# Decode key pages: loads from SyncE's queue, addressed by a register, in place of GpSimd's indirect row gathers

## The chip, the cores and the metric

The kernel runs on 1 core of one Trainium2 chip. The metric is the device time of one execution in microseconds (us), lower is better. The engines are named as in the profile: PE is TensorE (its weight loads are shown apart as PEld), DVE is VectorE, ACT is ScalarE, POOL is GpSimd, and SP is SyncE, which here only issues transfers; "SPq" in a row is such an issue.

## The reference

One step of a one-layer decoder trunk, in float32, for a prompt of 1024 tokens and for 8 sample sequences of one new token each. Prompt and samples share the weights. Each sample has 256 past tokens, whose keys and values lie in a cache of pages of 128 tokens; a page table names two pages for each sample. The part that matters here is the keys of the samples' differential attention:

```python
k_past = cache_k[l][page_table].reshape(Bd, past, H_A, 2 * DK_A)      # 8 samples, 256 tokens, 4 heads, 128
k_all = jnp.concatenate([k_past.astype(ka_d.dtype), ka_d], axis=1)
oa_d = diff_attention(qa_d, k_all, v_all, pos_d, kpos_d, rel_bias, lam)

def probs(qi, ki):
    s = jnp.einsum('bqhd,bkhd->bhqk', qi, ki).astype(f32) * scale + bias
    return jax.nn.softmax(jnp.where(mask, s, neg), axis=-1)

attn = probs(q1, k1) - lam * probs(q2, k2)
```

Around it stand the projections, the same attention and a retention over the prompt, a cross-attention into a memory, an MLP and several norms.

## The kernel before

The 1032 tokens (1024 of the prompt, 8 of the samples) are columns; weights come as "units" of 128 x 1024 floats. Each operand is split into a high part and a remainder (`wh`/`wl`, `UH`/`UL`, `KA`/`KB`, `VH`/`VL`), and each product is three matmuls. The program is written once, in one order; a scheduler places each engine's instructions from it, and within the attention stage (`pin[0] = True`) TensorE's are kept in the order written.

The attention stage runs from about 233 to 460 us. A loop over `g` from -4 to 39 takes the four heads, ten steps each (`items`): scores (`sp`, L1000), transposes (`trA`), weighting (`av`). Between them it feeds in a "filler": the projections of queries and keys of the next heads (`qkp`), and behind these the decode, `decode_steps`. Values of a head are fetched by SP into `vraw`, cast by ACT into `VH` (L974), and the remainder `VL` is formed on POOL (L976). Keys of a head are cast into `KA` by ACT (L948), the remainder `KB` is formed on DVE (L950), and both halves are copied across partitions by transfers that POOL issues (L949, L951). Weight units are loaded by SP into a pool of three buffers with the tag `raw`, cast by ACT (L128, `wh_u`) and their remainder is formed on DVE (L129, `wl_u`).

`decode_steps` builds an index tile `idk` of 128 x 16: column k holds 128 times the k-th page number plus the row. `fetch(x)` loads one of eight key tiles, each of two halves of 128 x 512 floats (256 KB), one page a half. The cache is laid out so that a page is 128 consecutive rows of 2 KB. Tiles 0 to 3 are fetched ahead, into the buffers of spent weight units; tiles 4 to 7 are fetched as the matmuls `dsc` consume tiles, into the `raw` buffers that vraw, a broadcast row (`rbh`) and, for the last one, tile 4 have used. Every half is one indirect DMA issued by POOL (`gather`, L858): POOL makes the row addresses, and the data goes over POOL's queue, q0. The other users of q0 in this stage are the copies of KA and KB and two loads of `UL` and `UH`.

SP issues its transfers strictly in order: one that waits for a buffer holds back what stands behind it. Its transfers carry one of eight semaphores in turn (`DMAHW0` to `DMAHW7`, those of POOL's queue `DMASW0` to `DMASW7`). Behind the attention stage the out-projection uses units that are loaded late in the stage (`raw_o`, L1396, and `raw_u`) and the stored head outputs `OP`, read back as `op` (L1258).

Of the kernel before, what the change touches and what calls it, by code (L numbers as in the profile page):

```python
# [12 lines left out]
I32 = mybir.dt.int32  # L13
AF = mybir.ActivationFunctionType
ALU = mybir.AluOpType
# [4 lines left out]
P = 128  # L20
# [28 lines left out]
def decoder_step(ctx: ExitStack, tc: tile.TileContext, i: dict, o: dict):  # L49
    nc = tc.nc  # L50

    def pool(name, bufs=1, space=None, side=None):
        if space is None:
            return tc.tile_pool(name=name, bufs=bufs, reuse_waits="tile", side=side)
        if space is PSUM:
            return tc.tile_pool(name=name, bufs=bufs, space=space, reuse_waits="tile")
        return tc.tile_pool(name=name, bufs=bufs, space=space)
# [111 lines left out]
    def bcast_rows(row_ap, p, n):  # L169
        return bass.AP(tensor=row_ap.tensor, offset=row_ap.offset, ap=[[0, p], [1, n]])  # L170
# [215 lines left out]
    with pool("a") as A:  # L386
# [250 lines left out]
        A = r_front.enter_context(pool("r", side="right"))  # L637
# [79 lines left out]
        for t in range(8):  # L717
# [33 lines left out]
            op = PS.tile([P, 512], F32, tag="op", name=f"op_{t}", bufs=2)  # L751
# [95 lines left out]
    def rep_rows(A, dt, src, nf, dst, nm, b0=0):  # L847

        for b in range(b0, b0 + nf // 4):
# [4 lines left out]
                nc.tensor.transpose(tp[:, x * P : x * P + P], ex.rearrange("p s g -> p (s g)"), ident)  # L854
            nc.scalar.copy(dst[:, b * 512 : b * 512 + 512], tp)

    def gather(raw, src, idx, k):
        nc.gpsimd.indirect_dma_start(  # L858
            out=raw, out_offset=None, in_=src, in_offset=bass.IndirectOffsetOnAxis(ap=idx[:, k : k + 1], axis=0)
        )  # L860
# [22 lines left out]
    with pool("b") as A:  # L883
# [243 lines left out]
        def decode_steps():  # L1127
# [8 lines left out]
            for j in range(2):  # L1136
                nc.vector.tensor_tensor(idx[:, 4 * j : 4 * j + 4], idx[:, 4 * j : 4 * j + 4],
                                        pt[:, j : j + 1].to_broadcast([P, 4]), op=ALU.add)
            idk = A.tile([P, 16], I32, tag="idk", name="idk")
            pos = A.tile([P, 1], I32, tag="pos", name="pos")  # L1140
            nc.sync.dma_start(idk, bcast_rows(i["page_table"], P, 16))
            nc.sync.dma_start(pos, i["pos"])
            nc.vector.tensor_scalar(idk, idk, 128.0, None, ALU.mult)
            nc.vector.tensor_tensor(idk, idk, pos.to_broadcast([P, 16]), op=ALU.add)
            sel = A.tile([64, 32], F32, tag="sel", name="sel")
            nc.sync.dma_start(sel, i["sel"])
            hm = A.tile([64, 5], F32, tag="hm", name="hm")
# [9 lines left out]
            raws2 = {}  # L1157

            def fetch(x):
                if x < 8:  # L1160
                    if x < 4:

                        raws2[x] = G.tile([P, 1024], F32R, tag="wl" if x % 2 else "wh", name=f"ck_0_{x}", bufs=RING).bitcast(F32)
                    else:
                        raws2[x] = G.tile([P, 1024], F32, tag="raw", name=f"ck_1_{x - 4}", bufs=3)
                    for y in range(2):
                        gather(raws2[x][:, y * 512 : y * 512 + 512], i["cache_kT"], idk, 4 * (x % 4) + 2 * y + x // 4)

            for x in range(4):
                fetch(x)  # L1170
                yield
# [101 lines left out]

        filler = head_proj(0)
        decode = decode_steps()

        def fill(n):
# [50 lines left out]
        for g in range(-4, 40):  # L1328
            h, x = divmod(g, 10)
# [70 lines left out]
            if g in UNITS_AT:  # L1400
                x = len(us_out)
# [5 lines left out]
        while len(us_out) < 4:  # L1407
            x = len(us_out)
# [622 lines left out]
    with pool("e") as A, pool("e_ps", space=PSUM) as PS:  # L2031
# [61 lines left out]
        for n, (ft, c) in enumerate(order):  # L2093
# [13 lines left out]
            x = xq[ft // 4, c][:, ft % 4, :]  # L2107
# [133 lines left out]
    with pool("acc", side="right") as AC, pool("rd", side="right") as RD, pool("w") as A, pool("w_ps", space=PSUM) as PS:  # L2241
# [105 lines left out]
        for g in range(4):  # L2347
# [26 lines left out]
            for new, qs, ps_ in parts:  # L2374
# [23 lines left out]
                for n, (q, p, c) in enumerate(steps):  # L2398
# [9 lines left out]
                    y = C[INTO[q]][:, p, cq]  # L2408
# [71 lines left out]
def _bucket(n):  # L2480
    n = np.maximum(n, 0)
    nf = np.maximum(n, 1).astype(np.float32)
    large = 16 + (np.log(nf / np.float32(16)) / np.float32(np.log(8.0)) * np.float32(16)).astype(np.int32)
    return np.where(n < 16, n, np.minimum(large, 31))


def _constants():
    f = np.float32
    c = {}
    c["ident"] = np.eye(P, dtype=f)  # L2490
    lg = np.log(f(1.0) - f(2.0) ** (f(-5.0) - np.arange(4, dtype=f))).astype(f)
    inv = (f(10000.0) ** (-np.linspace(0.0, 1.0, 32, dtype=f))).astype(f)
    pos = np.concatenate([np.arange(NT), np.full(P, 256)]).astype(f)
    ang = (pos[:, None] * inv[None, :]).astype(f)
    cos, sin = np.cos(ang), np.sin(ang)
    j = np.arange(P, dtype=f)
    dq = np.exp((j + 1)[:, None] * lg[None, :])
    dk = np.exp((127 - j)[:, None] * lg[None, :]) * f(0.125)
    rot = np.zeros((9, P, 2, 2, 4, 2, 32), f)
    for t in range(9):  # L2500
        cs, sn = cos[t * P : t * P + P], sin[t * P : t * P + P]
        for x, w in ((0, dq), (1, dk)):
            if t == 8:
                w = np.full((P, 4), 0.125 if x else 1.0, f)
            for h in range(4):
                for half in range(2):
                    rot[t, :, 0, x, h, half] = cs * w[:, h : h + 1]
                    rot[t, :, 1, x, h, half] = (sn if half else -sn) * w[:, h : h + 1]
    c["rot"] = rot.reshape(9, P, 1024)
    m = np.zeros((P, 4, P), f)  # L2510
    for h in range(4):
        m[:, h, :] = np.where(j[None, :] >= j[:, None], np.exp(f(-128.0) * lg[h]), 0)
    c["maskM"] = m.reshape(P, 512)
    rd = np.zeros((P, 2, 2), f)
    hs = np.zeros((P, 32), f)
    for p in range(2):
        for e in range(2):
            rd[64 * e : 64 * e + 64, p, 0] = np.exp(f(128.0) * lg[2 * p + e])
            rd[64 * e : 64 * e + 64, p, 1] = np.exp(lg[2 * p + e])
            hs[64 * e : 64 * e + 64, e] = 1  # L2520
    c["rdec"], c["hsel"] = rd, hs
    rel = 1023 - np.arange(BIASW)
    oh = np.zeros((33, BIASW), f)
    b = _bucket(rel)
    for x in range(BIASW):
        if rel[x] >= 0:
            oh[b[x], x] = -1
        else:
            oh[32, x] = 1
    c["onehot"] = oh  # L2530
    od = np.zeros((32, 257), f)
    od[_bucket(256 - np.arange(257)), np.arange(257)] = -1
    c["onehot_dec"] = od
    r = np.arange(64)
    c["sel"] = (r[:, None] % 32 == np.arange(32)[None, :]).astype(f)
    c["hm"] = np.concatenate([(r[:, None] % 32 // 8 == np.arange(4)[None, :]), r[:, None] >= 32], 1).astype(f)
    c["pos"] = np.arange(P, dtype=np.int32)[:, None]
    pp = np.arange(P)
    sg = (pp[None, :] // 16 == np.arange(8)[:, None]).astype(f)
    c["selg"], c["selgt"] = sg, np.ascontiguousarray(sg.T)  # L2540
    c["blk"] = (pp[None, :] // 16 == pp[:, None] // 16).astype(f)
    c["idxbase"] = ((pp % 16)[:, None] * 4 + np.arange(8)[None, :] % 4).astype(np.int32)
    return c


def _layout(x):
# [39 lines left out]
    d["cmk"] = a["cache_mem_k"].reshape(P, 16, 1024)  # L2586
    d["cmv"] = a["cache_mem_v"].reshape(P, 16, 1024)
    d.update(_constants())
    return {k: np.ascontiguousarray(v) for k, v in d.items()}

# [36 lines left out]
```

## Time and profile before

| | us |
|---|---|
| median of 3 runs | 1489.31 (1488.1 to 1490.61) |
| the profiled execution | 1496.69 |
| its span, first to last instruction | 1494.8 |
| granted TensorE clock, mean over the span | 0.995 |

Times in views are microseconds from the start of the span. A row of a timeline gives start, duration, engine, line, operation, output <- inputs, count, and in brackets the idle time of the engine ahead of it and what ended it. A row of stretches gives the busy time of PE, PEld, DVE, ACT and POOL, then the granted clock, the mean busy share of the 16 DMA engines and GB/s. A row of a tile's group gives the shortest, median and longest duration in ns. SP's queue before, around the places that the change touches, from its timeline:

```profile
373.03 0.32 SPq L937 DMA_DIRECT2D M<-brep  x1
384.17 0.28 SPq L1086 DMA_DIRECT2D hrow<-hr  x1
395.54 0.33 SPq L1119 DMA_DIRECT2D OP<-oraw  x1
423.87 0.33 SPq L122 DMA_DIRECT2D raw_u<-in_wall  x1
425.98 0.33 SPq L1258 DMA_DIRECT2D op<-OP  x1
```

### The profile page before, as it was taken

Reading aid. Unit: us, or ns where it says so; the run is one execution under the profiler, and the core shown is the slowest. Engines: PE = TensorE matmul, PEld = TensorE weight load, DVE = VectorE, ACT = ScalarE, POOL = GpSimd, SP = SyncE. Lnnn points to the kernel's source line nnn. Section 1 sums busy time; section 2 is a strip of 40 time slices with the busy share of each in tenths; the row PEclk is TensorE's granted clock in tenths of the full one; section 3 lists DMA queues with packets and bytes.
Section 4 is the critical chain, followed back from the end, with each engine's and each line's share of the span. In section 5 each row is a group of like instructions: output and inputs, shape, how many; then the busy total and the mean of one; then the engine's idle time right before and its main releaser. Section 6 shows DMA issues by size and latency. Waiting matters only on the chain.

```text
span 1494.8 us, 27880 instructions
## 1 busy us (share of the span) xinstructions
PE 1471.7 (98%) x10925; PEld 1401.8 (94%) x10925; DVE 1098.7 (73%) x2264; ACT 679.6 (45%) x1325; POOL 321.1 (21%) x346
## 2 busy tenths in 40 slices
PE   9999999998999999999999999999999999999997
PEld 7899779998779999989999999999999999999997
DVE  7666436887767636567886988888888879787865
ACT  7543435665552431248535643434334443343454
POOL 0035323123414311105022100000001311110380
PEclk9999999999999999999999999999999999999998
DMA  8255728213847157474582444344436774536273
GB/s 287 65 185 180 202 58 189 71 47 110 268 145 283 59 195 175 145 228 102 178 304 68 136 148 145 128 154 157 156 139 209 239 251 142 171 101 198 72 128 114
DMA packets 125238, 236.69 MB, mean 158 GB/s; under 512 B 13748, under 2 KB 76521, under 8 KB 124978
## 3 DMA queue, kind: packets, MB, share of 16 engines
q1 hardware_dynamic: 89064, 170.51, 36.0%
q0 software_dynamic: 24912, 44.80, 11.0%
q10 hardware_dynamic: 11130, 19.60, 3.5%
q8 instruction: 86, 1.41, 0.4%
q14 instruction: 46, 0.38, 0.1%
HBM read 170.25 MB, written 57.52 MB: 152 GB/s over the span
## 4 chain that ended last, share of the span: by engine, by line
PE 84%; DVE 8%; ACT 3%; issue 2%; DMA 2%; POOL 0%; ACTq 0%; another core or an unknown queue 0%; SPq 0%; DVEq 0%; POOLq 0%
PE dn L2309 19%; PE Z L2143 9%; PE qkp L75 7%; PE mq L75 6%; PE Y L2143 6%; PE X L2143 6%; PE pr_o L75 6%; PE pr_m L75 4%; PE grp L75 3%; PE sp L75 2%; PE av L75 2%; PE mv L75 1%; PE mk L75 1%; PE mpv L75 1%; PE vap_z L522 1%
## 5 line engine op out<-in xcount | busy, mean ns | idle before, releaser
L2309 PE MATMUL dn<-UH,wd 128*128 128x258 f32 x1792 | 325.1, 283 | 0.8 <-DVE c L2413 0.3
L2309 PEld LDWEIGHTS dn<-UH,wd 128*128 128x128 f32 x1792 | 277.6, 189 | 1.8 <-issue 0.8
L2309 PE MATMUL dn<-UL,wd 128*128 128x258 f32 x896 | 252.7, 282 | 0.0
L2309 PEld LDWEIGHTS dn<-UL,wd 128*128 128x128 f32 x896 | 169.0, 189 | 0.0
L2413 DVE TENSOR_TENSOR c<-c,dn 128x258 f32<-128x258 f32 x216 | 88.5, 417 | 38.2 <-PE dn L2309 35.8
L2169 ACT ACTIVATE hq<-r 128x258 f32<-128x258 f32 x128 | 53.9, 422 | 114.1 <-DVE r L2168 114.1
L2143 PE MATMUL X<-UH,wu 128*128 128x258 f32 x512 | 97.4, 282 | 0.9 <-ACT p L2194 0.9
L2143 PE MATMUL Z<-T_h,wu 128*128 128x258 f32 x512 | 98.2, 284 | 0.0
L2287 ACT CAST wd<-raw_d 128x512 fp32r<-128x512 f32 x96 | 58.8, 620 | 78.4 <-PE dn L2309 73.2
L1953 ACT CAST wu<-raw_up 128x512 fp32r<-128x512 f32 x96 | 59.2, 617 | 62.2 <-PE Z L2143 54.7
L2280 ACT CAST UH<-raw_h 128x1032 fp32r<-128x1032 f32 x56 | 58.8, 1057 | 55.0 <-PE dn L2309 27.3
L2143 PEld LDWEIGHTS X<-UH,wu 128*128 128x128 f32 x512 | 81.3, 188 | 1.1 <-ACT p L2194 1.1
L2143 PEld LDWEIGHTS Z<-T_h,wu 128*128 128x128 f32 x512 | 81.3, 189 | 0.0
L2281 DVE TENSOR_TENSOR UL<-raw_h,UH 128x1032 fp32r<-128x1032 f32 x56 | 73.4, 1311 | 9.9 <-ACT UH L2280 9.9
L2180 POOL DMA_DIRECT2D HT<-ht x32 | 17.2, 536 | 292.4 <-DVE ht L2179 291.9
L2288 DVE TENSOR_TENSOR wd<-raw_d,wd 128x512 fp32r<-128x512 f32 x96 | 72.0, 757 | 10.0 <-ACT wd L2287 9.9
L2143 PE MATMUL Z<-T_l,wu 128*128 128x258 f32 x256 | 72.3, 282 | 0.0
L2143 PE MATMUL X<-UL,wu 128*128 128x258 f32 x256 | 72.3, 282 | 0.0
L128 ACT CAST wh_u<-raw_u 128x1024 fp32r<-128x1024 f32 x43 | 44.7, 1049 | 54.2 <-PE mq L75 31.2
L1954 DVE TENSOR_TENSOR wu<-raw_up,wu 128x512 fp32r<-128x512 f32 x96 | 64.5, 684 | 3.7 <-ACT wu L1953 3.7
L129 DVE TENSOR_TENSOR wl_u<-raw_u,wh_u 128x1024 fp32r<-128x1024 f32 x39 | 51.6, 1328 | 18.3 <-ACT wh_u L128 18.1
L2301 POOL TENSOR_TENSOR raw_d<-raw_d,raw_d 128x512 f32<-128x512 f32 x16 | 22.1, 1382 | 194.5 <-DVE raw_d L2297 173.4
(598 smaller groups left out, 4718.2 us busy)
## 6 DMA issues: line engine op xcount, KB each, us to landing
raw_u<-in_wall SPq DMA_DIRECT2D x49, 512.0 KB
HT<-ht POOLq DMA_DIRECT2D x32, 516.0 KB
raw_h<-HT SPq DMA_DIRECT2D x32, 516.0 KB
raw_up<-in_wall SPq DMA_DIRECT2D x32, 512.0 KB
raw_d<-in_wall SPq DMA_DIRECT2D x32, 512.0 KB
HQ<-hq ACTq DMA_DIRECT2D x32, 387.0 KB
raw_h<-HQ SPq DMA_DIRECT2D x24, 516.0 KB
cmk<-in_cmk SPq DMA_DIRECT2D x16, 512.0 KB
```

The source lines that it names most:

```text
L75: pinned(nc.tensor.matmul(out, l, r, start=start, stop=stop))
L129: (lo_engine or nc.vector).tensor_sub(wl[:, :n], raw[:, :n], wh[:, :n].bitcast(F32))
L1953: nc.scalar.copy(w[:, :512], src)
L1954: nc.vector.tensor_sub(w[:, 512:], src, w[:, :512].bitcast(F32))
L2143: pinned(nc.tensor.matmul(ps, l, r[:, k, :], start=first and k == 0 and x == 0, stop=k == 3 and x == 2, skip_group_check=True))
L2169: nc.scalar.activation(h[:, PLACE[quad], :], r, AF.Square)
L2280: nc.scalar.copy(h, rv)
L2281: nc.vector.tensor_sub(l, rv, h.bitcast(F32))
L2287: nc.scalar.copy(w[:, :512], src)
L2288: nc.vector.tensor_sub(w[:, 512:], src, w[:, :512].bitcast(F32))
L2309: pinned(nc.tensor.matmul(ps, l, r[:, k, cq], start=first and k == 0 and x == 0, stop=k == 3 and x == 2, skip_group_check=True))
L2413: nc.vector.tensor_add(y, y, ps)
```

## The change

The index tile and its two operations on DVE go. The page table is loaded as one row of 16 numbers, and SP loads these into its registers. Each half of a key tile is then a plain transfer on SP's queue whose first row is 128 times the register; the range of the numbers is not checked at run time. Values are still gathered by POOL.

```diff
+    def page_numbers(A):
+
+        pg = A.tile([1, 16], I32, tag="idk", name="pg")
+        nc.sync.dma_start(pg, i["page_table"])
+        _, pages = nc.values_load_multi_w_load_instructions(
+            pg, engines=[mybir.EngineType.SP], min_val=0, max_val=i["cache_kT"].shape[0] // P - 1,
+            skip_runtime_bounds_check_because="the page table names pages of the cache")
+        return pages
...
-            idk = A.tile([P, 16], I32, tag="idk", name="idk")
-            pos = A.tile([P, 1], I32, tag="pos", name="pos")
-            nc.sync.dma_start(idk, bcast_rows(i["page_table"], P, 16))
-            nc.sync.dma_start(pos, i["pos"])
-            nc.vector.tensor_scalar(idk, idk, 128.0, None, ALU.mult)
-            nc.vector.tensor_tensor(idk, idk, pos.to_broadcast([P, 16]), op=ALU.add)
+            pages = page_numbers(A)
...
                     for y in range(2):
-                        gather(raws2[x][:, y * 512 : y * 512 + 512], i["cache_kT"], idk, 4 * (x % 4) + 2 * y + x // 4)
+                        pg = pages[4 * (x % 4) + 2 * y + x // 4]
+                        nc.sync.dma_start(raws2[x][:, y * 512 : y * 512 + 512], i["cache_kT"][bass.ds(pg * P, P), :])
```

What the scheduler makes of it, in three places. First, SP's queue where the first key tiles are fetched (`ck`; `rbh` is a broadcast row, `pg` the page numbers; in brackets the semaphores waited for). Before:

```order
L1091 DMA rbh_3596<-hrow 128x1024 [waits DMAHW5_49,DMAHW4_49,DMAHW2_49]
L964 DMA vraw_3607<-out_v_p 128x8x128 [waits DMAHW6_49]
L1119 DMA OP<-oraw_2751 128x1024 [waits DVE_49]
L937 DMA M_4038<-brep 128x1024 [waits DMAHW1_49,DVE_49]
L1086 DMA hrow<-hr_4174 8x128 [waits DMAHW0_49,Activation_49]
```

With the change:

```order
L1100 DMA rbh_3596<-hrow 128x1024 [waits DMAHW4_49,DMAHW3_49,DMAHW1_49]
L973 DMA vraw_3607<-out_v_p 128x8x128 [waits DMAHW5_49]
L861 TENSOR_LOAD pg [waits DMAHW3_49]
L1172 ISA
L1172 DMA ck_0_3948<-in_cache_kT 128x512 [waits PE_49]
L1172 ISA
L1172 DMA ck_0_3948<-in_cache_kT 128x512
```

The register load and eight key loads, each behind one register instruction (the first two are shown), stand between vraw and the store of OP.

Second, SP's queue where the last key tile (`ck_3_4627`) is fetched. Before, it isn't on this queue:

```order
L1119 DMA OP<-oraw_3284 128x1024 [waits DVE_49]
L1396 DMA raw_o_4557<-in_wall 128x1024 [waits DMASW5_49,DMAHW7_49,DMASW1_49,PE_49]
L1396 DMA raw_o_4561<-in_wall 128x1024 [waits DMASW6_49,DMASW2_49,PE_49]
L1396 DMA raw_o_4559<-in_wall 128x1024 [waits DMASW7_49,DMASW3_49,PE_49]
L1396 DMA raw_o_4563<-in_wall 128x1024 [waits DMASW4_49,DMAHW2_49,DMASW0_49,PE_49]
L122 DMA raw_u_5005<-in_wall 128x1024 [waits DMASW1_49,DMAHW3_49,DMASW0_49,PE_49]
L1258 DMA op_4586<-OP 128x1024 [waits DMAHW5_49,DMAHW6_49,DMAHW4_49,DVE_49]
```

With the change:

```order
L1172 DMA ck_2_4513<-in_cache_kT 128x512 [waits DMAHW3_49]
L1401 DMA raw_o_4586<-in_wall 128x1024 [waits DMASW5_49,DMAHW4_49,DMASW1_49,PE_49]
L1401 DMA raw_o_4590<-in_wall 128x1024 [waits DMASW6_49,DMAHW5_49,DMASW2_49,PE_49]
L1401 DMA raw_o_4588<-in_wall 128x1024 [waits DMASW7_49,DMAHW6_49,DMASW3_49,PE_49]
L1401 DMA raw_o_4592<-in_wall 128x1024 [waits DMASW4_49,DMAHW7_49,DMASW0_49,PE_49]
L1172 ISA
L1172 DMA ck_3_4627<-in_cache_kT 128x512 [waits DMAHW0_49,PE_49]
L1172 ISA
L1172 DMA ck_3_4627<-in_cache_kT 128x512 [waits DMAHW1_49]
L122 DMA raw_u_5034<-in_wall 128x1024 [waits DMAHW2_49,PE_49]
L1263 DMA op_4615<-OP 128x1024 [waits DMAHW3_49,DVE_49]
```

The last key tile waits for PE, behind the four loads of `raw_o` and ahead of the loads of `raw_u` and `op`.

Third, 100 us ahead of the first key tile, POOL's instructions for the first head: the value remainder `VL` and the copies of `KA` and `KB`. Before:

```order
L674 DMA OPL<-rl_2426 128x4x128
L976 TENSOR_TENSOR VL_2746<-vraw_2570,VH_2745 128x512 x2
L949 DMA KA_0_2511<-KA_0_2511 64x688
L951 DMA KB_0_2513<-KB_0_2513 64x688
L949 DMA KA_0_2512<-KA_0_2512 64x688
L951 DMA KB_0_2514<-KB_0_2514 64x688
```

With the change:

```order
L674 DMA OPL<-rl_2426 128x4x128
L958 DMA KA_0_2511<-KA_0_2511 64x688
L960 DMA KB_0_2513<-KB_0_2513 64x688
L958 DMA KA_0_2512<-KA_0_2512 64x688
L960 DMA KB_0_2514<-KB_0_2514 64x688
L985 TENSOR_TENSOR VL_2746<-vraw_2570,VH_2745 128x512 x2
```

`VL` moves behind the four copies, and ACT's two casts `VH` move behind its two casts `KA` in the same way. With that the `raw` buffers change hands in another order: the load `raw_u_2752` on SP, which waited for POOL (the buffer of `vraw`, free after `VL`), now waits for DVE and ACT (the buffer of a weight unit, free after L129), and the load behind it waits for POOL.

The order of PE's instructions doesn't change. On POOL the sixteen gathers go, and the load of `UH` (L1254) no longer stands behind two of them.

More of the change, by code (lines that the diff above doesn't have):

```diff
@@ L2536, in _constants @@
     c["hm"] = np.concatenate([(r[:, None] % 32 // 8 == np.arange(4)[None, :]), r[:, None] >= 32], 1).astype(f)
-    c["pos"] = np.arange(P, dtype=np.int32)[:, None]
     pp = np.arange(P)
```

## The prediction

> **What bounds the kernel now.** I read the first part of the page, then the busy time of the engines in stretches over the stages that the change touches, then the timelines of single engines, and last the chain of work.
>
> ```profile
> span 1494.8 us, 27880 instructions
> PE 1471.7 (98%) x10925; PEld 1401.8 (94%) x10925; DVE 1098.7 (73%) x2264; ACT 679.6 (45%) x1325; POOL 321.1 (21%) x346
> 240.00:260.00 20.00, 20.00 (x129) 19.83 (x128) 15.39 (x38) 12.80 (x27) 7.34 (x11) 1.00 0.85 204
> 260.00:280.00 20.00, 19.13 (x124) 18.32 (x123) 18.74 (x54) 12.23 (x26) 1.09 (x4) 1.00 0.13 36
> 345.00:350.00 5.00, 2.62 (x17) 2.26 (x15) 2.14 (x7) 1.13 (x3) 3.00 (x5) 1.00 0.97 307
> 350.00:355.00 5.00, 3.54 (x23) 3.26 (x23) 5.00 (x16) 3.84 (x9) 2.43 (x2) 1.00 0.20 77
> ```
>
> TensorE is busy 98% of the span: 1494.8 - 1471.7 = 23.1 us of idle is all that a change can take away without taking matmuls away, and this change takes none. GpSimd is busy 21%. So the question is which of the 23 us belong to the gathers, and whether anything new makes TensorE wait. The stretches (after the window: PE, weight loads, DVE, ACT, POOL, granted clock, DMA share, GB/s) show one large hole, 2.38 + 1.46 = 3.84 us between 345 and 355, in the middle of the first eight gathers, and 0.87 us between 260 and 280, where the vector engine is nearly full.
>
> **The change part by part: what leaves GpSimd.**
>
> ```profile
> L858 POOL DMA_INDIRECT ck<-in_cache_kT,idk x16: 945/974/1385, 337.6 to 421.3; - x16
> 394.76 1.04 PE L75 MATMUL dsc<-ck,qblkd 128*64 128x512 f32 x2
> 339.28 0.68 DVE L1034 TENSOR_TENSOR al<-trA,ah 128x512 fp32r<-128x512 f32 x1
> 336.26 0.69 DVE L1034 TENSOR_TENSOR al<-trA,ah 128x512 fp32r<-128x512 f32 x1
> ```
>
> Sixteen gathers of some 1.0 us leave GpSimd, 16 us. The first key tile is needed by the matmul at 394.76, 57 us after the first gather, and no wait of TensorE in the trace ends on a gather or a key tile. Nor does the vector engine get faster: the same subtraction took 0.68 us while a gather was being issued (339.28) and 0.69 us when none was (336.26). Worth: 0. The two index operations that leave the vector engine (some 0.35 us at 238) stand before an idle stretch of that engine. Worth: 0. The bytes that are moved stay the same.
>
> **What SyncE's queue gets.** It issues sixteen loads, one load of the page numbers into registers, and an instruction ahead of each load.
>
> ```profile
> 335.32 0.69 SPq L964 DMA_DIRECT2D vraw<-out_v_p  x1
> 337.64 1.06 POOL L858 DMA_INDIRECT ck<-in_cache_kT,idk  x1 [0.30 <-PE sp L75]
> 345.55 0.32 SPq L1119 DMA_DIRECT2D OP<-oraw  x1
> 388.11 0.33 SPq L1185 DMA_DIRECT2D qblkd<-in_onehot_dec  x1
> 394.81 0.33 SPq L1258 DMA_DIRECT2D op<-OP  x1
> ```
>
> A plain load costs the queue 0.3 to 0.7 us by these rows. The first eight stand behind vraw and ahead of the store of OP: between 336.0 and 345.5 the queue is idle, and it waits until some 337.3 for the first buffer, as GpSimd does now. The trace has no load into a register. From below it costs as one issue, 0.3; from above, as if each of the sixteen numbers cost the dearest issue here, 16 x 0.69 = 11 us. I take 0.3, since it is one instruction. Even at 11 us the loads end near 351, 44 us before the first matmul, and the OP behind them is read back at 394.81. The next two fit between 388.4 and 394.8. So 0 at both ends; the cover is gone only where the register load took over 30 us.
>
> The Trainium skill ("DMA: Bandwidth & Descriptors", section "Latency and other measured facts") puts the floor of such a register load at about 600 ns. No row here shows one; with it as the price of each of sixteen numbers the sum would stay the same, an estimate of 9.6 us, inside the bounds above.
>
> **The tightest place of the queue** is the last key tile, which waits for the matmul that frees its buffer and now stands behind four loads of 512 KB.
>
> ```profile
> 416.43 2.46 SPq L1396 DMA_DIRECT2D raw_o<-in_wall  x4
> 418.63 1.07 PE L75 MATMUL dsc<-ck,qblkd 128*64 128x512 f32 x2
> 430.23 1.07 PE L75 MATMUL dsc<-ck,qblkd 128*64 128x512 f32 x2
> 415.00:420.00 5.00, 5.00 (x25) 3.20 (x24) 4.89 (x16) 3.40 (x7) 0.02 (x1) 1.00 0.50 161
> 420.00:425.00 5.00, 4.63 (x24) 2.34 (x22) 3.82 (x9) 3.98 (x6) 2.46 (x5) 1.00 0.97 350
> ```
>
> The matmul frees the buffer at 419.7, so the two halves are issued by 420.5. Ahead of them lie 2.1 MB, of which 0.8 MB have moved by 420 (5 us at 161 GB/s); 1.3 MB and the tile's 0.5 MB at 350 GB/s take 5.2 us more, to 425.2. It is needed at 430.23: 5 us to spare. Worth: 0.
>
> **What moves by itself** is the only thing I charge. The order around 240 changes: the two value subtractions on GpSimd (VL) go behind the four copies of KA and KB, because their casts on ACT go behind those of KA.
>
> ```profile
> 241.11 2.54 POOL L976 TENSOR_TENSOR VL<-vraw,VH 128x512 fp32r<-128x512 f32 x2 [0.44 <-ACT VH L974]
> 242.49 1.56 ACT L948 CAST KA<-kraw 64x688 fp32r<-64x688 f32 x2 [0.94 <-DVE kraw L919]
> 245.81 0.52 POOL L951 DMA_DIRECT2D KB<-KB  x1
> 246.14 2.35 DVE L129 TENSOR_TENSOR wl_u<-raw_u,wh_u 128x1024 fp32r<-128x1024 f32 x2
> 264.00 0.41 PE L75 MATMUL sp<-KA,Q 128*128 128x320 f32 x1 [0.87 <-DVE mn L1000]
> 352.57 2.50 POOL L976 TENSOR_TENSOR VL<-vraw,VH 128x512 fp32r<-128x512 f32 x2 [2.95 <-ACT VH L974]
> 352.65 1.21 DVE L1014 SCALAR_TENSOR_TENSOR mn<-mn,nlam,sm 128x1 f32<-128x1 f32 x1
> 340.13 0.22 DVE L1014 SCALAR_TENSOR_TENSOR mn<-mn,nlam,sm 128x1 f32<-128x1 f32 x1
> 354.25 1.37 DVE L1015 SCALAR_TENSOR_TENSOR e<-e,mn,e 128x512 f32<-128x512 f32 x1
> 305.28 0.74 DVE L1015 SCALAR_TENSOR_TENSOR e<-e,mn,e 128x512 f32<-128x512 f32 x1
> ```
>
> VL ran from 241.1 to 243.6. Now it follows the last KB copy, at some 246.0 to 248.5, exactly beside the two weight subtractions (L129, from 246.14), which feed on two operands in SBUF. What that can cost is shown at 352.57: beside VL, L1014 took 1.21 us instead of 0.22, and L1015 1.37 instead of 0.74, each about as if it waited for one half of VL to end (1.25 us). The delay goes down the vector engine's queue (Q, kraw, the first score tiles) to 264.00, where TensorE already waits 0.87 us for it, so little of it is absorbed. Bounds: 0, where the subtractions start first and VL waits instead; 2.5, where they wait for both halves. In the rows the first half of VL starts about when the first subtraction does, and the engine still idles in 4.6 of the 20 us from 240 to 260 (the first of the stretches above), so I take one half, 1.25, less some slack: +0.8 us, nearer to the lower end.
>
> The Trainium skill ("SBUF — State Buffer", section "Who interferes with whom") says that a vector instruction with two SBUF inputs and a GpSimd instruction that reads SBUF shut each other out for a whole instruction, the later one waiting. The rows at 352.65 and 354.25 agree; by that rule alone the cost here would be one or two halves of VL, or none, by who issues first.
>
> Behind the same wait stands a weight load on SyncE's queue, which now waits for L129 instead of VL.
>
> ```profile
> 236.29 0.38 SPq L964 DMA_DIRECT2D vraw<-out_v_p  x1
> 240.40 1.14 ACT L974 CAST VH<-vraw 128x512 fp32r<-128x512 f32 x2 [1.66 <-DMA vraw<-out_v_p]
> 243.67 4.04 SPq L122 DMA_DIRECT2D raw_u<-in_wall  x2
> 251.97 1.05 ACT L128 CAST wh_u<-raw_u 128x1024 fp32r<-128x1024 f32 x1
> ```
>
> It goes out at about 247.4 instead of 243.67. By vraw, 240.40 - 236.29 = 4.1 us from issue to use for 512 KB, it is there at 251.5; its cast runs at 251.97. Half a us to spare: 0, and where the subtractions are late, the cast is late with them.
>
> **The sum.** In the profiled execution's own time, 1496.69 us (span 1494.8 and 1.9 around it), this is 1496.69 + 0.8 = 1497.5. That execution lies 7.4 us above the median of the runs shown, 1489.31, and the rival below is about what these 7 us are. Against the median: 1489.31 + 0.8 = **1490.1**; I say 1490. With 0 to 2.5 and the spread of the runs (1488.1 to 1490.6) the forecast's own range is 1488 to 1492.5. About 0.2%, 3 us, is what a measurement of this kernel can tell from no change.
>
> **Rival 1, faster: the hole at 346 is made by the gathers, in every run.**
>
> ```profile
> 349.34 0.69 DVE L1000 CUSTOM_DVE_ANT_0 e<-sp,M 128x512 f32<-128x512 f32 x1 [2.86 <-remote]
> 350.09 0.41 PE L75 MATMUL sp<-KA,Q 128*128 128x320 f32 x1 [2.47 <-DVE mn L1000]
> 345.97:349.38 3.41, 1.66 (x12) 1.37 (x10) 0.55 (x4) 0.71 (x2) 2.01 (x3) 1.00 1.00 304
> 352.80:356.20 3.40, 1.36 (x10) 1.07 (x9) 3.26 (x7) 1.40 (x3) 2.27 (x2) 1.00 0.00 0
> 356.20:359.60 3.40, 3.40 (x15) 3.40 (x14) 3.00 (x10) 1.41 (x3) 0.00 (x0) 0.50 0.00 0
> ```
>
> The vector engine stands for 2.86 us on something that the trace cannot name, GpSimd is just issuing its last first-batch gathers, and DMA is full. The price is the 3.84 us of the hole and half of the 3.4 us at clock 0.50 behind it, 1.7: 5.5 us, giving 1490.1 - 5.5 = 1484.6. For it: the place. Against it: the eight later gathers make no such hole, and the excess of the profiled execution, 7.4 us, is what a hole that only this execution had would leave. Chance 0.18.
>
> **Rival 2, slower: VL holds the vector engine twice, and the clock drops.** The price is the upper bound, 2.5 us, and 1.7 more if TensorE's wait near 264 then empties a clock window. The rows above give the point: with 1.66 us of work in 3.41 the clock stayed at 1.00, with 1.36 in 3.40 it fell to 0.50. So over about 1.9 us of idle in one such window decides, 0.87 there now and 1.0 more. Time: 1489.31 + 4.2 = 1493.5. For it: VL and L129 meet almost to the tenth. Against it: the wait would have to fall into one window, and TensorE has work in between. Chance 0.13.
>
> **Rival 3: the last key tile comes late,** if the queue moves 2.6 MB slower than reckoned; it decides from 430.23 on, that is below some 190 GB/s from 416.4, and then costs its lateness, 3 us at 155 GB/s: 1493. The page has 350 GB/s there. Chance 0.05. That the loads do not leave GpSimd at all is excluded by the order.
>
> **How the numbers follow.** Forecast 0.62 (no change), rival 1 0.18 (faster), rivals 2 and 3 0.18 (slower), 0.02 left over. Of the forecast's cases with VL near 2.5 a few pass 3 us, of rival 1's, some stay within it: faster 0.18, same 0.64, slower 0.18. The range 1484.3 to 1493.2 takes in most of rival 1 and rival 2's lower part and leaves out some 0.15.
>
> **What will show it.** Right: VL near 246 with L129 longer than 2.35 us in sum or VL longer than 2.5; the wait near 264 between 0.9 and 3 us; the key loads on SyncE's queue before 351, 395 and 421, and no wait of TensorE on a key tile. Wrong: a hole near 346 again without a gather (rival 1 is dead) or in both kernels' unprofiled difference 5 us (it lives); a clock of 0.50 near 264; a dsc matmul after 430 released by a DMA.

## Result, and the profile after

Over 22 runs of each kernel, the kernel before took 1488.07 us in the median (1485.72 to 1490.61) and the changed kernel 1490.6 (1489.07 to 1493.21). The ratio is 1.0018, with a 95% interval of 1.0012 to 1.0024: 2.7 us, or 0.2%, slower (2.5 us by the medians). The profiled execution of the changed kernel took 1491.67 us, where that of before took 1496.69. So the two profiles differ by 5 us in favour of the change and the timed runs by 2.5 us against it; this contradiction is the main thing to explain. One thing can be seen at once: the profiled execution of the changed kernel is one of its 22 runs, that of before is not one of its own, all of which lie below 1491.

From the first part of the page after:

```profile
span 1489.9 us, 27898 instructions
PE 1469.2 (99%) x10925; PEld 1400.0 (94%) x10925; DVE 1098.3 (74%) x2262; ACT 677.9 (45%) x1325; POOL 304.7 (20%) x330
```

TensorE is idle for 20.7 us instead of 23.1. The busy time by stretches after, columns as in the prediction (the stages lie some 3 us later in this execution by 345):

```profile
240.00:260.00 20.00, 19.06 (x120) 18.37 (x119) 15.77 (x30) 11.55 (x24) 6.75 (x10) 1.00 0.74 197
260.00:280.00 20.00, 18.20 (x108) 17.43 (x107) 17.27 (x53) 10.79 (x24) 0.35 (x2) 0.91 0.09 28
262.69:266.10 3.41, 1.61 (x11) 1.35 (x10) 3.41 (x10) 1.18 (x3) 0.00 (x0) 1.00 0.21 31
266.10:269.51 3.41, 3.41 (x15) 3.35 (x14) 1.57 (x7) 2.00 (x4) 0.00 (x0) 0.51 0.30 123
345.00:350.00 5.00, 5.00 (x35) 4.79 (x34) 4.87 (x13) 2.27 (x7) 0.38 (x2) 1.00 1.17 301
350.00:355.00 5.00, 4.27 (x31) 3.98 (x30) 5.00 (x17) 4.46 (x12) 2.10 (x2) 1.00 0.72 271
```

Two things changed, with opposite signs. From 240 to 280, where 0.87 us were idle, 0.94 + 1.80 = 2.74 us are idle now, and the clock falls to about half behind it, from 266.1 to 269.5. And the hole of 3.84 us between 345 and 355 has shrunk to 0.73. The rows behind both, from the timeline after:

```profile
245.36 2.55 POOL L985 TENSOR_TENSOR VL<-vraw,VH 128x512 fp32r<-128x512 f32 x2
245.37 4.77 DVE L129 TENSOR_TENSOR wl_u<-raw_u,wh_u 128x1024 fp32r<-128x1024 f32 x2
251.09 0.38 PE L75 MATMUL sp<-KA,Q 128*128 128x256 f32 x1 [0.54 <-DVE Q L966]
256.31 0.45 PE L75 MATMUL sp<-KA,Q 128*128 128x384 f32 x1 [0.40 <-DVE mn L1009]
265.62 0.41 PE L75 MATMUL sp<-KA,Q 128*128 128x320 f32 x1 [1.79 <-DVE mn L1009]
341.47 6.75 SPq L1172 DMA_DIRECT2D ck<-in_cache_kT  x8
386.68 1.00 SPq L1172 DMA_DIRECT2D ck<-in_cache_kT  x2
393.65 7.57 SPq L1172 DMA_DIRECT2D ck<-in_cache_kT  x4
417.29 1.03 SPq L1172 DMA_DIRECT2D ck<-in_cache_kT  x2
430.12 1.07 PE L75 MATMUL dsc<-ck,qblkd 128*64 128x512 f32 x2
```

POOL starts VL at 245.36 and the first L129 starts 0.01 us later; the two L129 take 4.77 us in sum instead of 2.35. TensorE waits for DVE in three places, 0.54 + 0.40 + 1.79 = 2.73 us. The key loads are out by 348.2, 387.7, 401.2 and 418.3, and the dsc row of the last key tile has no wait in front.

**A ruler.** Spans of different executions also differ elsewhere by some us, so I measure the two places by themselves: stretch A from a matmul ahead of 240 (`sc`) to one behind 330 (`hrT`), and stretch B from there to a transpose near 420. TensorE's order is the same in all these kernels. Before and after:

```profile
211.64 1.13 PE L75 MATMUL sc<-qblk,kT 128*128 128x256 f32 x4 [0.65 <-DVE kT L726]
333.14 0.27 PE L78 MATMUL hrT<-ident,c 128*8 128x128 f32 x1 [0.27 <-DVE c L1067]
424.47 0.55 PE L78 MATMUL trA<-ident,e 128*128 128x128 f32 x3 [0.37 <-DVE e L1015]
```

```profile
210.91 1.13 PE L75 MATMUL sc<-qblk,kT 128*128 128x256 f32 x4 [0.66 <-DVE kT L726]
336.31 0.27 PE L78 MATMUL hrT<-ident,c 128*8 128x128 f32 x1 [0.26 <-DVE c L1076]
422.03 0.55 PE L78 MATMUL trA<-ident,e 128*128 128x128 f32 x3 [0.38 <-DVE e L1024]
```

A is 121.50 us before and 125.40 after: 3.9 us lost, of which up to 1.7 by the 3.41 us at half clock. B is 91.33 before and 85.72 after: 5.6 us gained. Together that is 1.7 us in favour of the change; the other 3.2 us by which the two spans differ lie outside both stretches, 0.7 ahead of A and 2.5 behind B. The same two stretches for all profiles of this study, by start times of the same rows (the kernels are described below):

| kernel | chip | A | B |
|---|---|---|---|
| before | | 121.50 | 91.33 |
| before, again | I | 122.40 | 91.25 |
| change | | 125.40, half clock | 85.72 |
| change, again | II | 123.91 | 85.75 |
| loads, old order | I | 121.50 | 85.74 |
| loads, old order, again | II | 121.44 | 85.79 |
| gathers, new order | I | 125.38, half clock | 91.27 |
| loads, VL twice | I | 126.38, half clock | 85.77 |
| loads, one half of VL | III | 122.59 | 85.73 |
| loads, values first | III | 121.42 | 85.71 |
| gathers, values first | III | 122.32 | 85.71 |
| gathers for tiles 0 to 3 | II | 121.95 | 85.75 |
| gathers for tiles 4 to 7 | II | 124.70, half clock | 85.70 |

The kernels ran in three groups, each on another chip (I, II, III), each timed beside the kernel before; its median was 1492.8 us on chip I, 1487.35 on II and 1487.78 on III. One run of it on chip I took 4195.87 us and is left out of the ratios. On which chip the two profiles without a chip in the table were taken isn't known. Ratios are to the kernel before on the same chip.

### The profile page after: what moved, and what is told of

It reads as the page before. It is cut to its first block, busy times and chain, and to the rows that moved or that the text cites. A ratio compares the mean times of both kernels' runs of the same rounds, so it can differ in the third digit from the quotient of the medians.

```text
span 1489.9 us, 27898 instructions
## 1 busy us (share of the span) xinstructions
PE 1469.2 (99%) x10925; PEld 1400.0 (94%) x10925; DVE 1098.3 (74%) x2262; ACT 677.9 (45%) x1325; POOL 304.7 (20%) x330
## 4 chain that ended last, share of the span: by engine, by line
PE 85%; DVE 8%; ACT 3%; issue 2%; DMA 2%; POOL 0%; ACTq 0%; DVEq 0%; POOLq 0%; SPq 0%
PE dn L2314 19%; PE Z L2148 9%; PE qkp L75 7%; PE mq L75 6%; PE Y L2148 6%; PE X L2148 6%; PE pr_o L75 5%; PE pr_m L75 4%; PE grp L75 3%; PE sp L75 2%; PE av L75 2%; PE mv L75 2%; PE mk L75 1%; PE mpv L75 1%; PE vap_z L522 1%
## 5 line engine op out<-in xcount | busy, mean ns | idle before, releaser
L129 DVE TENSOR_TENSOR wl_u<-raw_u,wh_u 128x1024 fp32r<-128x1024 f32 x39 | 51.8, 1334 | 18.0 <-ACT wh_u L128 17.7
L75 PE MATMUL qkp<-UH,wh_u 128*128 128x344 f32 x192 | 63.2, 329 | 0.1
```

The costliest lines, as they stand in the source:

```text
L75: pinned(nc.tensor.matmul(out, l, r, start=start, stop=stop))
L129: (lo_engine or nc.vector).tensor_sub(wl[:, :n], raw[:, :n], wh[:, :n].bitcast(F32))
```

## The experiments

### Order and transport apart

The change moves the transport (gathers to loads) and, through the scheduler, the order near 240. The first kernel keeps the loads and restores the order, only by writing the load of the page numbers some lines further down:

```diff
-            pages = page_numbers(A)
             sel = A.tile([64, 32], F32, tag="sel", name="sel")
...
                     relb.unsqueeze(2).to_broadcast([32, 4, 8]),
                 )
+            pages = page_numbers(A)
             raws2 = {}
```

> The change, with its page-number load written a few lines further down, so that the order on DVE and ACT is that of before and POOL forms VL of the first head ahead of the copies of KA and KB again. Theory 1 (the whole loss is VL beside the weight subtractions of L129): the two L129 near 246 take 2.35 us in sum again instead of 4.77, TensorE waits about 0.9 us near 264 instead of 2.7 in three places, and the time is that of before, 1488.1 +- 0.6 us. Theory 2 (the loads on SyncE's queue cost something by themselves: the 2.0 us register load, the eight issues ahead of the store of OP, the later last key tile): the order changes nothing of that, and the time stays at 1490 to 1491. Theory 3 (the gathers make a hole near 346 in every run): below 1486, since the gathers are gone and the collision too.

Measured on chip I: 1487.42 us against 1492.8, ratio 0.9971 (0.9961 to 0.9980). So the time that theory 1 named was met within 0.1 us, but it was not "that of before", which was 4 to 5 us longer on this chip. As a difference from before it is nearer to what theory 3 named, the hole of the gathers; that comes below. The second kernel keeps the gathers and takes the new order:

```diff
                 nc.scalar.copy(KA[m][own, cs], kraw[own, cs])
+                seen["KA"] = nc.cur_bb.bb.instructions[-1]
...
         for _ in load_part(0, EARLY):
             pass
+        first_KA = seen["KA"]
...
                 if x == 0:
-                    load_values(h)
+                    with tc.issue_after(first_KA) if h == 0 else nullcontext():
+                        load_values(h)
```

> The kernel before, gathers kept on POOL, but the casts VH of the first head are issued behind those of KA, so that VL stands behind the copies of KA and KB as in the changed kernel; nothing else moves. Theory 1: L129 near 246 takes some 4.8 us in sum, TensorE waits 2.7 us between 250 and 266, and the time is 1490.6 +- 0.6 us, as with the change. Theory 2: no loads on SyncE's queue, so 1488.1 as before.

Measured on chip I: 1495.81 us against 1492.8, ratio 1.0019 (1.0007 to 1.0030). Its timeline near 246:

```profile
246.26 2.54 POOL L977 TENSOR_TENSOR VL<-vraw,VH 128x512 fp32r<-128x512 f32 x2
246.28 4.75 DVE L129 TENSOR_TENSOR wl_u<-raw_u,wh_u 128x1024 fp32r<-128x1024 f32 x2
```

With no load on SyncE's queue the same collision appears and the same loss: the order alone costs what the change costs, and stretch A is 125.38 us as against 125.40 in the change, each with one window at half clock. Theory 2 falls. The time itself, 1490.6 by theory 1, was missed by 5 us, about as much as the kernel before took longer on this chip than in the first comparison (4.7).

On chip II the change and the loads with the old order ran side by side:

> The change itself, beside the kernel before on the same chip as the two below. In the first comparison it was 2.5 us slower than before; since then the kernel before took 1492.8 us in one comparison and 1488.1 in another, while kernels without gathers stayed within a us or two. Theory A (two effects: VL beside L129 costs 2 to 3.5 us always, and the gathers' hole near 347 costs up to 5.3 us, but not on every chip or in every session): where before takes 1492 to 1493, the change takes 1490 to 1491 and is faster; where before takes 1488, it is slower. Theory B (the hole is only in profiled executions): slower by 2.5 us wherever it is run.

> The change with the old order near 240 once more, on the chip of the three above. VL away from L129: 2.5 to 3.3 us below the change in the same session, whatever the kernel before takes; if its gain over before was an accident of the other session, it is now equal to before.

Measured: the change 1490.71 us, ratio 1.0021 (1.0012 to 1.0030); with the old order 1488.21, ratio 1.0004 (0.9995 to 1.0013); before 1487.35. The order is worth 1490.71 - 1488.21 = 2.5 us, the loss of the first comparison, and what is left of the change cannot be told from nothing. Between the theories A and B this pair does not decide: where before takes 1487, both name a loss. Timelines of the change again, and of the old order:

```profile
210.57 1.13 PE L75 MATMUL sc<-qblk,kT 128*128 128x256 f32 x4 [0.66 <-DVE kT L726]
245.07 4.76 DVE L129 TENSOR_TENSOR wl_u<-raw_u,wh_u 128x1024 fp32r<-128x1024 f32 x2
265.32 0.42 PE L75 MATMUL sp<-KA,Q 128*128 128x320 f32 x1 [1.78 <-DVE mn L1009]
334.48 0.27 PE L78 MATMUL hrT<-ident,c 128*8 128x128 f32 x1 [0.26 <-DVE c L1076]
```

```profile
210.65 1.13 PE L75 MATMUL sc<-qblk,kT 128*128 128x256 f32 x4 [0.65 <-DVE kT L726]
240.03 2.54 POOL L985 TENSOR_TENSOR VL<-vraw,VH 128x512 fp32r<-128x512 f32 x2
245.12 2.35 DVE L129 TENSOR_TENSOR wl_u<-raw_u,wh_u 128x1024 fp32r<-128x1024 f32 x2
262.96 0.41 PE L75 MATMUL sp<-KA,Q 128*128 128x320 f32 x1 [0.84 <-DVE mn L1009]
332.09 0.27 PE L78 MATMUL hrT<-ident,c 128*8 128x128 f32 x1 [0.25 <-DVE c L1076]
```

Stretch A is 123.91 against 121.44: 2.47 us, with no fall of the clock in either. DVE's two L129 differ by 4.76 - 2.35 = 2.41 us. The delay passes down to TensorE whole.

### How long DVE waits for POOL

If VL holds L129, the hold should follow the number of VL instructions. One kernel forms each half twice, one moves the second half away:

```diff
-                eng.tensor_sub(VL[:, cs], vraw[:, cs], VH[:, cs].bitcast(F32))
+                for _ in range(2 if h == 0 else 1):
+                    eng.tensor_sub(VL[:, cs], vraw[:, cs], VH[:, cs].bitcast(F32))
```

> The changed kernel, with each half of VL of the first head formed twice by POOL (four instructions of 1.27 us instead of two), the same result. Theory 1 (each vector instruction with two SBUF operands waits for one VL instruction that got there first): the two Q subtractions behind L129 wait for the other two, 2.5 us more on DVE, all of it paid by TensorE since no slack is left there: 1493.1, and up to 1.7 more if the clock drops in every run instead of some. Theory 2 (VL is not what holds L129, but a late operand or the queue): as the changed kernel, 1490.6.

```diff
                 nc.gpsimd.dma_start(KB[m][oth, cs], KB[m][own, cs])
+                seen["KB"] = nc.cur_bb.bb.instructions[-1]
...
-                eng.tensor_sub(VL[:, cs], vraw[:, cs], VH[:, cs].bitcast(F32))
+                with tc.issue_after(seen["KB"]) if h == 0 and cs.start else nullcontext():
+                    eng.tensor_sub(VL[:, cs], vraw[:, cs], VH[:, cs].bitcast(F32))
```

> The changed kernel, with the second half of VL of the first head put behind the copies of KA and KB of the late columns, some 8 us later, so that one VL instruction instead of two (the change) or four (VL twice) stands at the place of L129. Theory 1a (one vector instruction with two SBUF operands waits for everything that POOL issues back to back): the first L129 takes 1.21 + 1.26 = 2.5 us, between the 3.63 of the change and the 1.21 without VL beside it. Theory 1b (it waits for a fixed time, or for the last of the copies): 3.6 us as in the change.

The groups of L129 (shortest, median, longest duration in ns; the longest is the one that waited) with VL's row above: with two VL instructions (the change), with four, and with one.

```profile
L129 DVE TENSOR_TENSOR wl_u<-raw_u,wh_u x2: 1214/2422/3630, 245.4 to 248.9; 128x1024 fp32r<-128x1024 f32 x2
```

```profile
245.26 5.04 POOL L986 TENSOR_TENSOR VL<-vraw,VH 128x512 fp32r<-128x512 f32 x4
L129 DVE TENSOR_TENSOR wl_u<-raw_u,wh_u x2: 1212/3663/6114, 245.3 to 251.3; 128x1024 fp32r<-128x1024 f32 x2
```

```profile
245.13 1.31 POOL L987 TENSOR_TENSOR VL<-vraw,VH 128x512 fp32r<-128x512 f32 x1
L129 DVE TENSOR_TENSOR wl_u<-raw_u,wh_u x3: 1212/1224/2382, 245.2 to 253.2; 128x1024 fp32r<-128x1024 f32 x3
```

The first L129 takes 1.21 us with no VL beside it, 2.38 with one, 3.63 with two and 6.11 with four: 1.2 us for each VL instruction, and always the first L129 bears all of it. My expectation for four, that the Q subtractions behind would wait for the other two, was wrong in this: here the engines do not take turns. Elsewhere they do. In the second profile of before (described below) the two halves of VL stand beside the two KB subtractions:

```profile
L976 POOL TENSOR_TENSOR VL<-vraw,VH x2: 1290/1604/1917, 242.3 to 243.5; 128x512 fp32r<-128x512 f32 x2
L950 DVE TENSOR_TENSOR KB<-kraw,KA x2: 883/1371/1859, 243.4 to 244.3; 64x688 fp32r<-64x688 f32 x2
```

The first KB subtraction started some 0.1 us ahead of VL's second half and took 0.88 us, as it does alone; VL's second half was the one that waited, 1.92 us instead of 1.29, and the second KB subtraction waited for that. So DVE got in between two instructions of POOL there. What lets POOL keep its place for its whole row beside L129 these runs do not show.

Stretch A follows the doses, 1.15 and 4.94 us above the 121.44 of the old order where DVE's L129 are 1.17 and 4.90 longer (3.52 and 7.25 in sum). The kernel with four has a window at half clock in A too, from 254.7, but TensorE waits for DVE once more behind it, 0.93 us at 268.01, so that DVE's delay alone sets the end; in the change the window comes behind the last wait and adds to it. The kernel with one half was only profiled, at 1488.79 us. With four VL the time was 1493.94 us on chip I, ratio 1.0004 (0.9994 to 1.0015), within the 1493.1 to 1494.8 that was expected; that this equals before there is the subject of the next part.

### The hole near 347

> The kernel before once more, for a second profile. If the hole of 3.8 us between 345 and 355 with the drop of the clock behind it belongs to the gathers, it is there again; if it was an accident of the first profile, TensorE's wait near 350 is gone and the profiled time is some 5 us under 1496.7.

It was there again, on chip I, at 1494.43 us. From the timeline of that kernel:

```profile
349.78 0.69 DVE L1000 CUSTOM_DVE_ANT_0 e<-sp,M 128x512 f32<-128x512 f32 x1 [2.13 <-PE sp L75]
350.53 0.42 PE L75 MATMUL sp<-KA,Q 128*128 128x320 f32 x1 [2.28 <-DVE mn L1000]
```

So it was no accident of one execution. The other gather kernel on that chip, with the new order, has it too (B 91.27), and the two load kernels there lack it (85.74, 85.77). To find which gathers make it, I split them:

```diff
-                        pg = pages[4 * (x % 4) + 2 * y + x // 4]
-                        nc.sync.dma_start(raws2[x][:, y * 512 : y * 512 + 512], i["cache_kT"][bass.ds(pg * P, P), :])
+                        k = 4 * (x % 4) + 2 * y + x // 4
+                        if x < 4:
+                            gather(raws2[x][:, y * 512 : y * 512 + 512], i["cache_kT"], idk, k)
+                        else:
+                            nc.sync.dma_start(raws2[x][:, y * 512 : y * 512 + 512], i["cache_kT"][bass.ds(pages[k] * P, P), :])
```

with the index tile kept beside the page numbers, and the other kernel with `x >= 4`.

> Tiles 0 to 3 by gathers on POOL, tiles 4 to 7 by loads on SyncE's queue, the order near 240 as before. If the hole belongs to the first eight gathers, it is there in the profile (DVE and POOL standing until about 1 us after the last gather, TensorE idle some 4 us between 345 and 360, a clock of 0.50 behind it), and the time is that of before within 1 us.

> The other half: tiles 0 to 3 by loads, tiles 4 to 7 by gathers, order near 240 as before. If the hole belongs to the first eight gathers, it is gone: TensorE idle under 1.2 us between 345 and 360, and the time is that of the all-loads kernel with the old order, 1487.5 +- 0.7 us, 4 us under before if before takes 1492, the same if before takes 1488.

These ran on chip II, and the first expectation failed: the hole was in neither (B 85.75 and 85.70), although the first eight gathers are issued in the first kernel as before:

```profile
347.66 0.96 POOL L867 DMA_INDIRECT ck<-in_cache_kT,idk  x1 [0.30 <-issue]
346.72 0.68 DVE L1009 CUSTOM_DVE_ANT_0 e<-sp,M 128x512 f32<-128x512 f32 x1
241.87 2.54 POOL L985 TENSOR_TENSOR VL<-vraw,VH 128x512 fp32r<-128x512 f32 x2 [1.87 <-ACT VH L983]
243.21 2.83 DVE L959 TENSOR_TENSOR KB<-kraw,KA 64x688 fp32r<-64x688 f32 x2 [0.83 <-ACT KA L957]
```

DVE's row at 346.72 has no wait. So the split tells nothing of which gathers matter. Neither time came out as expected: the kernels took 1489.27 us, ratio 1.0014 (1.0005 to 1.0023), and 1489.08, ratio 1.0007 (0.9998 to 1.0017), so the first is 2 us slower than before without the hole and without VL at L129. Its last two rows show a part of the cause: VL runs only from 241.87, and the KB subtractions beside it take 2.83 us, against 1.93 in the loads with the old order on the same chip. It is the same collision, one place earlier. But stretch A is only 0.5 us longer for it (121.95 against 121.44); the rest of the 2 us no profile shows. In the second kernel VL runs even later, from 243.07; the copy of KA stands behind it, TensorE waits 1.50 us for that copy, and a window at half clock follows (A 124.70).

This collision goes with vraw: its issue lies 25.35 and 25.76 us behind the start of stretch A in these two kernels and 25.51 in the second profile of before, which has the collision too (A 122.40), but 24.63 to 24.93 in all the others. That profile of before has no additional small load, so such a load alone is not what made vraw late; what did stays open.

### Out of vraw's way

So I tried to take vraw out of the race in both kernels: the small loads of the decode go behind it (the other kernel has the same edit with `idk` and `pos`).

```diff
+            with tc.issue_after(seen["V"]):
                 pt = A.tile([P, 2], I32, tag="pt", name="pt")
                 nc.sync.dma_start(idx, i["idxbase"])
...
                 nc.sync.dma_start(relb, i["rel_bias"])
```

> The changed kernel, with the values of the first head (vraw) issued ahead of the six small loads of the decode on SyncE's queue instead of behind them. Its casts then come ahead of those of KA, so VL is formed ahead of the copies of KA and KB, and nothing depends on the last us of vraw any more. Theory (the loss is only VL's place): KB 1.8 us, L129 2.35 us in sum, TensorE waits 0.9 us near 264, and the time is that of the loads with the old order, 1487.4 to 1488.2 in the two earlier sessions, or up to 0.5 us less: 2.5 us or more below the change. If the six loads, now later, hold up DVE through pt, hm and relb, it is slower than that by what DVE then waits ahead of 242.

> The same move in the kernel before, gathers kept: the pair with the kernel above differs in gathers against loads alone, with vraw out of the way in both. If the gathers cost nothing outside the session in which the hole near 347 appeared: equal to the loads within 0.6 us where before takes 1487 to 1488; where before takes 1492 or more, this one is 4 to 5 us slower than the loads, and the hole is in its profile.

Measured on chip III: loads 1487.82 us, ratio 0.9999 (0.9991 to 1.0008); gathers 1488.47, ratio 1.0006 (0.9998 to 1.0015); before 1487.78. B is 85.71 in both: sixteen gathers, no hole. Loads and gathers can't be told apart here by their times, and neither kernel beats before. (Stretch A differs, 121.42 and 122.32, so the two are not equal near 240; why was not looked into.) The vraw transfer left no earlier for the move, at 235.48, 24.64 us behind the start of stretch A (210.84), where the loads with the old order had it at 235.30, 24.65 behind theirs (210.65). So the small loads had not been what it waited for.

A version that is faster than both kernels everywhere did not come out. Loads with the old order are faster than the change on chip II, and equal to before there; on chip I they are 4.3 us faster than before.

## Why the prediction was right in its number, and where it was wrong

**Gathers off POOL, 0.** Right on chips II and III: with the order held, loads and gathers differ by less than the measurement tells (1.0004; 0.9999 beside 1.0006). Wrong on chip I, below.

**SyncE's queue, 0.** Right. From the profile of the change:

```profile
L861 SPq TENSOR_LOAD <-pg x1: 2011/2011/2011, 339.2 to 339.2; - x1
SPq L1172 <- DMA vraw<-out_v_p: 2.5, 1, 2.5
```

The register load took 2.01 us, far nearer to the lower bound of 0.3 than to the upper of 11. The issues took 0.33 to 0.37 us each, the lower part of the 0.3 to 0.7 taken. Of the 6.75 us of the first eight loads 2.5 are a wait of the last one for vraw, which I had not reckoned with; the rest is 0.53 us each, register instructions included. None of TensorE's waits behind them ends on SyncE's queue or on a key tile.

**The last key tile, 0.** Right: issued at 417.29, used at 430.12 without a wait.

**VL behind KA and KB, +0.8.** The mechanism and the place were right, the size was wrong by a factor of three; this is the step that failed. I had taken one half of VL, 1.25 us, from rows near 352, less some slack. In place of that the first L129 waited for both halves, 2.4 us, as the doses 1.21, 2.38, 3.63 and 6.11 us show, and no slack absorbed any of it: 2.47 us in stretch A without a fall of the clock. My rows near 352 were no measure for this. There L1014 started 0.08 us into the first half of VL and ended with it, at 353.86, though a second half followed; L1015 started in the second half, behind which no third stood. One half was a fair reading of them, but L129, 0.01 us behind the first of two, waited for both. What makes that difference is not shown. The upper bound, 2.5, was the truth, and the term alone would have given 1488.07 + 0.8 = 1488.9 where 1490.6 was measured. That the number 1490.0 still lies so near 1490.6 is half luck: I had set out from 1489.31, and the kernel before was 1488.07 over more runs, so a start 1.2 us too high hid most of a term 1.7 us too small.

**The Trainium skill on the collision.** "SBUF — State Buffer", section "Who interferes with whom", gives the pair of ports that the two engines share to whoever issues first, for the whole instruction. The runs agree that POOL, 0.01 us ahead, held DVE. Beside L129 it held DVE over all of its instructions that stand back to back; beside KB, in the second profile of before, DVE got in between.

**Rival 2, slower.** Its first half is what happened. Its second, the clock, happened in the profiled execution: 1.61 us of work in 3.41 and then the clock at 0.51, near 264, which I had named as a sign of being wrong. In the change on chip II the clock did not fall, with waits of the same size (1.78 near 265). The Trainium skill ("TensorE: Matmul & The Clock Gate", section "What's actually happening") says that the windows run free of the kernel's start; a fall in one execution and not in another with the same waits agrees with that. In the profiled execution the wait of 1.79 lies within one window. In the change on chip II, counted back in steps of 3.413 us from 1479.12, where its clock fell at the end, it lies across an edge at 263.97, and the two windows hold 2.98 and 2.06 us of work. How often the clock fell here in the timed runs is not known. The granted clock was 0.998 in 11 of the changed kernel's 22 runs, which took 1489.9 us in the mean, and 0.996 or 0.997 in the other 11, with 1491.4; but the kernel before spans the same clocks on chip III, and its profile has a window at half clock from 786.29, far from this place. My point, 1.9 us of idle in one window, does not hold as a rule:

```profile
250.24:253.65 3.41, 1.82 (x11) 1.36 (x10) 2.44 (x5) 1.42 (x4) 0.59 (x2) 1.00 1.23 250
263.17:266.58 3.41, 1.71 (x13) 1.59 (x12) 3.30 (x11) 0.79 (x2) 0.00 (x0) 1.00 0.43 131
782.88:786.29 3.41, 3.15 (x28) 3.06 (x27) 0.63 (x3) 1.26 (x5) 1.09 (x2) 1.00 0.14 48
```

The clock fell to 0.50 behind the first (gathers for tiles 4 to 7) and the third (before), and stayed at 1.00 behind the second (gathers, values first), which has the least work of the three. So TensorE's busy time in these rows is not enough to tell when the clock falls; what decides is not shown.

**Rival 1, the hole of the gathers.** I gave it 0.18 and a price of 5.5 us, and priced it well: 5.6 us by stretch B, gone wherever loads stand at this place. But it is not in every run, which the rival said, nor was it an accident of one execution, which I argued against it: the first profile of before and the two profiles with gathers on chip I have it, but neither of the two with gathers at this place on II and III. Timed runs speak for the same split: before took 1492.8 us on chip I, 5.4 us over its own time on II, while the loads with the old order took 1487.42 and 1488.21 on the same two chips. In the first comparison, where before took 1488.07, the timed runs can hardly have had it while the page shows it. That resolves the signs of the contradiction at the start: the profile of before carries 5.6 us that the timed runs beside it lacked, and the change loses its 2.5 us in both. The difference of 5 us itself is a sum, 5.6 by the hole, less 3.9 in stretch A, and 3.2 elsewhere; of the 3.2, up to 1.7 are the window at half clock from 786.29, which the profile of the change lacks. On chip I the change itself was not run; by its parts, 4.3 us gained and 2.5 lost, it should be some 2 us faster than before there, an estimate.

**What stays open.** Why the hole appears on one chip and not on two others, with the same gathers at the same place, was not found; whether it goes with the chip or with the session isn't known either: there is one session on each chip. Its size in timed runs is argued from medians, not seen.

## What to carry to other kernels

A small edit can leave its own cost at zero and still cost time through the order that a scheduler makes of it: compare the orders, and look for vector instructions with two operands in SBUF that come to stand beside POOL's arithmetic, then reckon with up to the whole row of POOL's back-to-back instructions, not with one of them. Where two profiles and two medians disagree in sign, cut the trace at matmuls that both kernels share and compare stretch by stretch before explaining a span. And time kernels beside each other on the same chip, on more than one: here one stall of 5.6 us belonged to some sessions only.

## What the hardware showed that I had not expected

In the hole, DVE and POOL wait for TensorE, whose matmuls stand more than 3 us earlier in the trace. The trace also records when TensorE's signals arrive (the semaphore that both wait for); in the kernel before and in the loads with the old order on chip I, around the same scores:

```
before:           344.85 345.61 | 349.22 349.26 349.32 349.38 349.46 349.51 349.55
loads, old order: 347.09 347.56 347.85 348.14 349.21 349.32 350.09 350.38
```

Before, no signal comes for 3.6 us, then seven in 0.33 us, while TensorE's rows show it working until 347.6. So the signals, or the ends of the matmuls behind them, were held up while POOL issued gathers. A gap of 3.1 us stands ahead of this one (341.73 to 344.85). The other two profiles with the hole show such gaps too, with the new order from 345.96 to 349.60, for instance; the two with gathers and without the hole have the same row of gathers and no gap above 1.3 us in that place. What held the signals the traces do not show.
